# Streaming encoder layer on one core: unsplit stores for attention outputs and normed rows, in-place splits on load, low parts of weights on VectorE, two buffers for squares

## The chip, the cores and the metric

The kernel runs on one core of one Trainium2 chip. The metric is device time in microseconds (us) for one execution of the whole program; the comparison is by the median of several executions. Engine names are those of the profile: PE is TensorE's matmul stream, PEld its weight loads, DVE is VectorE, ACT is ScalarE, POOL is GpSimd, SP is SyncE. In this kernel SP issues all large transfers.

## The reference

One layer of a streaming encoder, in float32, for a prompt of 2048 rows and a sample of 32 rows with model width 1024 (2080 columns together):

```
h  = rmsnorm(x);  qa,ka,va,qb,kb,vb,g_low,r = split(h @ w_in)
oa = chunk-band attention(qa,ka,va)        # 8 heads x 64, own chunk and 8 before
ob = gated linear attention(qb,kb,vb,...)  # 4 heads, key 64, value 128
x  = x + rmsnorm(concat(oa, norm(ob)*g*silu(r)) @ w_o)
mk, mv = rmsnorm(mem) @ w_mk, rmsnorm(mem) @ w_mv          # 256 memory tokens
x  = x + rmsnorm(attention(rmsnorm(x) @ w_mq, mk, mv) @ w_mo)   # 4 heads x 256
h2 = rmsnorm(x)
x  = x + rmsnorm((silu(h2 @ w_gate) * (h2 @ w_up)) @ w_down)    # hidden 2816
```

It returns the new rows, the newest keys and values, the states of the linear attention and the memory keys and values.

## The kernel before

**Products.** Data lie feature-major: 128 features on the partitions, rows of the sequence along the free axis. A float32 operand is used as two parts, a high part, which is a rounded copy, and a low part, which is the operand less its high part; a product is three matmuls (high by high, high by low, low by high), issued at L485. `split` (L426, L430) makes the parts: ACT casts the high one (L426), and DVE or POOL subtracts for the low one (L430). Which of the two subtracts is the list `lo_set`, gone through in turn: POOL and DVE alternate in the projections, in cross attention and in the FFN, POOL alone in the stage between. Projections and FFN products multiply 2 by 2 blocks in seven products (X, Y, Z are their sums in PSUM); the combinations of weight blocks that this needs are additions and subtractions on DVE (L529, L532).

**Stages of the profiled execution.** Projections of three column blocks, 0 to 609 us (`wva`, `wvb`, `wqa`, `wka`, `wr`, `wqb`, `wkb` are their weights, `mi` the normed input in two parts). Then, 609 to 1425 us, band attention, the linear attention, the memory's keys and values, the output projection (`wops<-om,wo_s`, four column blocks) and the first memory query. Cross attention, 1425 to 1915 us, goes over five blocks of 416 columns (`m` the normed rows, `wmq`, `wmo` weights, `mpr` the exponentials of the scores). The FFN, 1915 to 3374 us, has three column blocks of 11 groups: gate (`pg<-mf,wg_s`), up (`pu<-mf,wu_s`) and down (`pdn<-u,wd`); `mf` is the normed input in two parts, `acc` the output block, two halves at a time.

**What passes through memory.** Attention outputs go to `od` and the normed rows of the first residual to `h1d`, each stored as a high and a low array and loaded as both: `om` loads `od` (128 x 2 x 512), `hq` and `m` load `h1d`. The names that are split for this are `o`/`os` and `g_sg`/`g_obs` (for `od`) and `y`/`h` (for `h1d`): an ACT cast, a POOL subtraction and two stores for each tile. The normed rows of the FFN go unsplit through `h2d` (L1704) and come back as `hr` (L1754).

**Order of issue.** The class `Order` reads every instruction of the program, gives each a time from a formula (`_cost`, L84), and runs a list scheduler forward and backward, `PASSES` times; the best schedule's order is written into the program as the order of issue on each engine, SP's queue included. Each engine then takes its instructions strictly in that order and waits at the head of its queue.

**End of an FFN block.** Squares of the output (`sq`, one buffer, L1854) are summed on DVE into `ssq` (L532); a matmul with ones gives `n_ps` (L1889), ACT makes the factor `n_r` (L434, L435), DVE multiplies it into `acc` (L1896, 16 tiles), and POOL adds the residual (`x2r`). Until a half of `acc` is stored, the next block's first results (`acc<-pdn`, L571) for that half wait.

Of the kernel before, what the change touches and what calls it, by code (L numbers as in the profile page):

```python
# [18 lines left out]
P = 128  # L19
D = 1024  # L20
# [27 lines left out]
class Order:  # L48
# [8 lines left out]
    GATE = 5  # L57
    SLOW = 1.0
    PASSES = 6

# [23 lines left out]
    def _cost(self, ins, kind, eng, outs, inps):  # L84
# [169 lines left out]
    def _pass(self, prio, back=None):  # L254
# [35 lines left out]
        while True:  # L290
            again = True
            while again:
                again = False
                for e, heap in enumerate(ready):
                    while idle[e] and heap:
# [27 lines left out]
                        if back is None:  # L323
                            seen = fin + lat[i]
                            if e == 4:
                                moved = max(moved, fin) + lat[i]
                                seen = max(fin + 2800.0, moved + 2500.0)
                            end[i] = seen
                            heappush(events, (seen, 1, i))
                        else:  # L330
                            end[i] = fin
# [4 lines left out]
            while events and events[0][0] <= now:  # L336
# [7 lines left out]
                for j in nxt[i]:  # L344
                    same = eng[j] == eng[i] and eng[i] != 4
                    if back is None:
                        if same == (kind == 0):
                            left[j] -= 1
                            if not left[j]:
                                heappush(ready[eng[j]], (prio[j], j))  # L350
                    else:
                        left[j] -= 1
                        if not left[j]:
                            heappush(events, (now + (0.0 if same else 3000.0 if eng[j] == 4 else lat[j]), 2, j))
                if last:
# [38 lines left out]
def encoder_step(ctx, tc, ins, outs):  # L394
# [26 lines left out]

    flip = [0]
    lo_set = [[nc.gpsimd, nc.vector, nc.gpsimd]]

    def split(hi, lo, src, lo_eng=None):
        ACT.copy(hi, src)  # L426
        if lo_eng is None:
            flip[0] += 1
            lo_eng = lo_set[0][flip[0] % len(lo_set[0])]
        lo_eng.tensor_tensor(out=lo, in0=src, in1=hi.bitcast(F32), op=ALU.subtract)  # L430

    def rstd_of(pool, ps_ap, n, count, name, bufs=2):
        r = pool.tile([P, n], F32, tag="rstd", name=name, bufs=bufs)
        ACT.activation(r, ps_ap, AF.Ln, bias=eps_t, scale=1.0 / count)  # L434
        ACT.activation(r, r, AF.Exp, scale=-0.5)  # L435
        return r
# [67 lines left out]
    sgd = [dpool.tile([512, n], F32, name=f"sgd{b}") for b, (_, n) in enumerate(PBLK)]  # L504
    od = [dpool.tile([D, 2, n], F32, name=f"od{b}") for b, (_, n) in enumerate(BLK)]
    x1d = [dpool.tile([D, n], F32, name=f"x1d{b}") for b, (_, n) in enumerate(BLK)]
    h1d = [dpool.tile([D, 2, n], F32, name=f"h1d{b}") for b, (_, n) in enumerate(BLK)]
    mkd = dpool.tile([D, NMEM], F32, name="mkd")
# [64 lines left out]

    lo_set[0] = [POOL, DVE]
    WCH = 1056
# [369 lines left out]

    lo_set[0] = [POOL]
    wph = ctx.enter_context(ExitStack())
    wp = wph.enter_context(tc.tile_pool(name="wpool", bufs=4, **RW))
    with ExitStack() as ph:
# [52 lines left out]
        def load_mov(src, n, name, order=range(KT)):  # L1002
            mv = {}
            for k in order:
                mv[k] = mp.tile([P, 2, 544], F32R, tag="mov", name=f"{name}_{k}")
                SP.dma_start(mv[k][:, :, :n].bitcast(F32), src[k * P : (k + 1) * P])
            return mv
# [67 lines left out]

        def heads_out(dst, osb, n, name):

            hi = lp.tile([P, 256], F32R, tag="osr", name=name, bufs=2)
            split(hi[:, :n], osb[:, :n].bitcast(F32R), osb[:, :n], POOL)
            SP.dma_start(dst[:, 0], hi[:, :n].bitcast(F32))  # L1080
            SP.dma_start(dst[:, 1], osb[:, :n])

        nbs = {}
# [14 lines left out]
        def band_group(t0, c):  # L1098
# [17 lines left out]
            def unit(tt, e):  # L1116
# [22 lines left out]
                def third():  # L1139
                    if e == 0:  # L1140
                        g["po"] = po_.tile([P, 512], F32, tag="po", name=f"po{t}_{c}")
                    values(g["po"], g["v"][:, k0 // P : k0 // P + nkt], u["prt"], [P] * nkt, e, P)
                    if e:
                        take(g["osb"][:, tt * P : (tt + 1) * P], g["po"], P, f"rec{t}_{c}")
                        if tt:
                            (b, lo, hi, _), = pieces(BLK, t0 * P, t0 * P + 256)
                            heads_out(od[b][c * P : (c + 1) * P, :, lo:hi], g["osb"], 256, f"os{t}_{c}")

# [4 lines left out]
        def band_sample(c):  # L1153
# [20 lines left out]
            def unit(e):  # L1174
# [12 lines left out]
                def third():  # L1187
# [19 lines left out]
        def gla_tile(tk, n, st, name):  # L1207
# [117 lines left out]
            DVE.tensor_tensor(out=sg[:, :, :n], in0=tts[:, :, :n], in1=sg[:, :, :n], op=ALU.mult)  # L1325
            hi = gp.tile([P, 4, P], F32R, tag="obs", name=name + "_obs")
            split(hi[:, :, :n], sg[:, :, :n].bitcast(F32R), sg[:, :, :n], POOL)
            for i, src in enumerate((hi.bitcast(F32), sg)):
                SP.dma_start(od[b][512:1024, i, lo:hi_].rearrange("(h p) n -> p h n", p=P), src[:, :, :n])

# [14 lines left out]
        def out_proj(b):  # L1345
# [101 lines left out]
        def mem_q0():  # L1447
# [277 lines left out]
    with ExitStack() as ph:  # L1725
# [92 lines left out]
        for b, (s, n) in enumerate(CF):  # L1818
# [28 lines left out]
            def square(ci, m):  # L1847
# [37 lines left out]
            def finish(ci, xrs, b=b, s=s, n=n, acc=acc, ssqs=ssqs, last=b == len(CF) - 1, load_x2=load_x2):  # L1885
# [155 lines left out]
```

## Time and profile before

| | |
|---|---|
| median of 3 executions | 3371.97 us (3369.83 to 3383.44) |
| the profiled execution | 3376.22 us |
| its span, first to last instruction | 3374.4 us |
| mean granted TensorE clock | 0.970 |
| bytes moved by DMA | 520.42 MB |
| POOL's low parts of FFN weights (`wu_s`, `wg_s`, `wd`) | 205.2, 149.0, 91.5 us busy |
| SP queue, rows in the order of issue | 1757 |

In the quoted rows, the first number of a timeline row is the start in us from the span's start and the second the time it took; a square bracket is the idle time of that engine just ahead, with what ended it. A row of a table by windows has the window, its length, then busy us and count of PE, PEld, DVE, ACT and POOL, then the granted clock of TensorE (1.00 is full), the DMA engines' share and GB/s. A row of a group has busy us and the mean ns of one, then the idle time of the engine just before them and its releasers.

### The profile page before, as it was taken

Reading aid. Unit: us, or ns where it says so; the run is one execution under the profiler, and the core shown is the slowest. Engines: PE = TensorE matmul, PEld = TensorE weight load, DVE = VectorE, ACT = ScalarE, POOL = GpSimd, SP = SyncE. Lnnn points to the kernel's source line nnn. Section 1 sums busy time; section 2 is a strip of 40 time slices with the busy share of each in tenths; the row PEclk is TensorE's granted clock in tenths of the full one; section 3 lists DMA queues with packets and bytes.
Section 4 is the critical chain, followed back from the end, with each engine's and each line's share of the span. In section 5 each row is a group of like instructions: output and inputs, shape, how many; then the busy total and the mean of one; then the engine's idle time right before and its main releaser. Section 6 shows DMA issues by size and latency. Waiting matters only on the chain. (4 is left out here: it accounts for less than half of the span.)

```text
span 3374.4 us, 58279 instructions
## 1 busy us (share of the span) xinstructions
PE 3201.7 (95%) x21387; PEld 3046.6 (90%) x21387; DVE 2350.8 (70%) x4089; ACT 1725.3 (51%) x3718; POOL 1568.0 (46%) x1331
## 2 busy tenths in 40 slices
PE   7888999899999999889999799999989999899998
PEld 6788899788888788889999689999989999899998
DVE  7884865477677677377776886666876667866665
ACT  4554655465676666455556453334533334543334
POOL 3653533274345546554451654444454445544442
PEclk8999999799999999999999899999999999999999
DMA  5549364687586867877664632222242222322222
GB/s 140 170 130 298 115 192 129 226 257 230 181 286 194 256 193 233 279 241 226 198 187 129 199 118 76 76 77 73 91 143 76 75 76 76 117 88 75 76 76 93
DMA packets 520111, 520.42 MB, mean 154 GB/s; under 512 B 81936, under 2 KB 450745, under 8 KB 519825
## 3 DMA queue, kind: packets, MB, share of 16 engines
q1 hardware_dynamic: 519825, 516.70, 48.8%
q8 instruction: 168, 2.75, 0.3%
q14 instruction: 118, 0.97, 0.1%
HBM read 386.82 MB, written 130.87 MB: 153 GB/s over the span
## 5 line engine op out<-in xcount | busy, mean ns | idle before, releaser
L485 PE MATMUL pdn<-u,wd 128*128 128x346 f32 (+1 forms) x3168 | 521.8, 324 | 18.3 <-DVE acc L571 13.2
L485 PEld LDWEIGHTS pdn<-u,wd 128*128 128x128 f32 x3168 | 510.5, 190 | 21.1 <-DVE acc L571 14.7
L426 ACT CAST wg_s<-wg_r 128x512 fp32r<-128x512 f32 x231 | 139.5, 620 | 449.9 <-DVE wg_r L529 161.4
L430 POOL TENSOR_TENSOR wu_s<-wu_r,wu_s 128x512 fp32r<-128x512 f32 x132 | 205.2, 1563 | 276.0 <-ACT wu_s L426 244.9
L532 DVE TENSOR_TENSOR acc<-acc,pdn 128x346 f32<-128x346 f32 (+1 forms) x464 | 236.0, 514 | 136.5 <-PE pdn L485 136.0
L430 POOL TENSOR_TENSOR wg_s<-wg_r,wg_s 128x512 fp32r<-128x512 f32 x99 | 149.0, 1507 | 331.2 <-ACT wg_s L426 329.9
L485 PE MATMUL pg_X<-mf,wg_s 128*128 128x346 f32 (+1 forms) x1584 | 279.1, 323 | 18.0 <-ACT wg_s L426 14.9
L485 PE MATMUL pu_X<-mf,wu_s 128*128 128x346 f32 (+1 forms) x1584 | 275.9, 321 | 0.8 <-POOL wu_s L430 0.8
L485 PEld LDWEIGHTS pg_X<-mf,wg_s 128*128 128x128 f32 x1584 | 257.3, 189 | 20.9 <-ACT wg_s L426 15.6
L485 PEld LDWEIGHTS pu_X<-mf,wu_s 128*128 128x128 f32 x1584 | 256.0, 189 | 1.8 <-POOL wu_s L430 1.4
L1340 PE MATMUL wops<-om,wo_s 128*128 128x512 f32 (+1 forms) x960 | 225.2, 373 | 12.6 <-ACT wo_s L426 6.7
L485 PE MATMUL mops<-mo,wmo_s 128*128 128x416 f32 x960 | 200.0, 357 | 3.2 <-DVE y L1684 3.2
L1340 PEld LDWEIGHTS wops<-om,wo_s 128*128 128x128 f32 x960 | 156.6, 197 | 36.0 <-ACT wo_s L426 7.5
L485 PEld LDWEIGHTS mops<-mo,wmo_s 128*128 128x128 f32 x960 | 178.8, 190 | 7.2 <-ACT n_sq L445 3.5
L426 ACT CAST wu_s<-wu_r 128x512 fp32r<-128x512 f32 x231 | 134.3, 619 | 67.1 <-DVE wu_r L529 33.8
L1064 PE MATMUL po<-prt,v 128*128 128x128 f32 x1120 | 164.7, 287 | 2.8 <-DVE o L1074 2.3
L430 POOL TENSOR_TENSOR u<-sg,u 128x346 fp32r<-128x346 f32 (+1 forms) x132 | 140.0, 1071 | 52.5 <-ACT u L426 52.5
L485 PE MATMUL mqps<-m,wmq_s 128*128 128x416 f32 x768 | 161.4, 356 | 0.0
L1064 PEld LDWEIGHTS po<-prt,v 128*128 128x128 f32 x1120 | 150.3, 199 | 11.4 <-DVE o L1074 2.7
L485 PE MATMUL pu_Y<-mf,wu_s 128*128 128x346 f32 (+1 forms) x792 | 140.8, 323 | 7.1 <-ACT wu_s L426 4.6
L485 PEld LDWEIGHTS mqps<-m,wmq_s 128*128 128x128 f32 x768 | 140.0, 189 | 1.7 <-issue 0.5
L485 PE MATMUL pg_Y<-mf,wg_s 128*128 128x346 f32 (+1 forms) x792 | 138.4, 322 | 2.1 <-POOL wg_s L430 1.4
(476 smaller groups left out, 7949.7 us busy)
## 6 DMA issues: line engine op xcount, KB each, us to landing
wg_r<-in_w_ffn_gate_dram SPq DMA_DIRECT2D x66, 512.0 KB, 4.3
wu_r<-in_w_ffn_up_dram SPq DMA_DIRECT2D x66, 512.0 KB, 4.3
wd_r<-in_w_ffn_down_dram SPq DMA_DIRECT2D x66, 512.0 KB, 3.4
wmq_r<-in_w_mq_dram SPq DMA_DIRECT2D x80, 256.0 KB, 3.0
wmo_r<-in_w_mo_dram SPq DMA_DIRECT2D x80, 256.0 KB, 3.4
q<-qd SPq DMA_DIRECT2D x32, 512.0 KB, 4.3
wo_r<-in_w_o_dram SPq DMA_DIRECT2D x64, 256.0 KB, 4.3
om<-od SPq DMA_DIRECT2D x24, 512.0 KB, 8.2
```

The lines of the kernel that those rows point to most:

```text
L426: ACT.copy(hi, src)
L430: lo_eng.tensor_tensor(out=lo, in0=src, in1=hi.bitcast(F32), op=ALU.subtract)
L485: PE.matmul(ps, lhsT=a, rhs=b, start=first and i == 0, stop=last and i == len(seq) - 1, skip_group_check=skip)
L532: eng.tensor_tensor(out=out, in0=a, in1=b, op=ALU.add)
L1064: PE.matmul(po[:, e * P : e * P + n], lhsT=v[:kk, j, e * 64 : e * 64 + P], rhs=prt[:kk, j, :n], start=j == 0, stop=j == len(rows) - 1)
L1340: PE.matmul(ps, lhsT=a, rhs=b, start=i == 0, stop=i == len(seq) - 1)
```

## The change

1. `split` always subtracts on DVE unless an engine is named; `lo_set` is gone. By the order of issue some 620 subtractions go from POOL to DVE, among them `wu` 132, `wg` 99, `wd` 66, `wo` 64, `wmq` 48, `wmo` 40, and 21 each of `wva`, `wvb`, `wqa`, `wka`, `wr`.
2. `od` and `h1d` are stored unsplit. The casts and subtractions for them (48 for `od`, 32 for `h1d`, and those of the sample) go, and so does one of each two stores.
3. The loads `om` (32 tiles), `hq` (8) and `m` fetch one array and split it in place (`split_own`): an ACT cast, then a subtraction on DVE for even tiles and on POOL for odd ones.
4. Squares at the end of an FFN block have two buffers. The factor `r` no longer has a buffer of its own but takes one of these two.
5. The planner's numbers: `SLOW`, `PASSES`, the cost of a transfer and the latencies it assumes for one.

```diff
-    SLOW = 1.0
-    PASSES = 6
+    SLOW = 1.02
+    PASSES = 7
-            return 560.0, 1.05 * total / row * (8 + 0.148 * row) / 16
+            return 540.0, total / row * (8 + 0.18 * row) / 16
-                                seen = max(fin + 2800.0, moved + 2500.0)
+                                seen = max(fin + 2500.0, moved + 2200.0)
 ...
     def split(hi, lo, src, lo_eng=None):
         ACT.copy(hi, src)
-        if lo_eng is None:
-            flip[0] += 1
-            lo_eng = lo_set[0][flip[0] % len(lo_set[0])]
-        lo_eng.tensor_tensor(out=lo, in0=src, in1=hi.bitcast(F32), op=ALU.subtract)
+        (lo_eng or DVE).tensor_tensor(out=lo, in0=src, in1=hi.bitcast(F32), op=ALU.subtract)
+    def split_own(m, on_pool):
+        ACT.copy(m[:, 0], m[:, 1].bitcast(F32))
+        (POOL if on_pool else DVE).tensor_tensor(out=m[:, 1], in0=m[:, 1].bitcast(F32), in1=m[:, 0].bitcast(F32), op=ALU.subtract)
 ...
-                SP.dma_start(mv[k][:, :, :n].bitcast(F32), src[k * P : (k + 1) * P])
+                SP.dma_start(mv[k][:, 1, :n].bitcast(F32), src[k * P : (k + 1) * P])
+                split_own(mv[k][:, :, :n], k % 2)
 ...
-            hi = lp.tile([P, 256], F32R, tag="osr", name=name, bufs=2)
-            split(hi[:, :n], osb[:, :n].bitcast(F32R), osb[:, :n], POOL)
-            SP.dma_start(dst[:, 0], hi[:, :n].bitcast(F32))
-            SP.dma_start(dst[:, 1], osb[:, :n])
+                            SP.dma_start(od[b][c * P : (c + 1) * P, lo:hi], g["osb"])
 ...
-                    hi = sp.tile([P, 544], F32R, tag="st", name=f"h1_{b}_{k}")[:, :n]
-                    split(hi, ys[k].bitcast(F32R), ys[k], POOL)
-                    SP.dma_start(h1d[b][k * P : (k + 1) * P, 0], hi.bitcast(F32))
-                    SP.dma_start(h1d[b][k * P : (k + 1) * P, 1], ys[k])
+                    SP.dma_start(h1d[b][k * P : (k + 1) * P, :], ys[k])
 ...
-                    sq = small(np_, "nsq", f"sq{b}_{ci}_{m}", 1)[:, :n]
+                    sq = small(np_, "nsq", f"sq{b}_{ci}_{m}", 2)[:, :n]
-                r = rstd_of(np_, psn[:, :n], n, D, f"n5_{b}_{ci}_r", 1)
+                r = rstd_of(np_, psn[:, :n], n, D, f"n5_{b}_{ci}_r", 2, "nsq", 348)
```

With other numbers and other instructions the planner writes another order. Four places of it follow; in the rows, `out<-in` are tiles, the ending number tells tiles apart, and the line numbers of the changed kernel are a little smaller (L425 is its `split`'s subtraction, L424 its cast, L429 the cast of `split_own`).

POOL's first arithmetic before, in the first projection block, is low parts of the weights `wva` and of the input `mi`:

```order
L430 TENSOR_TENSOR wva_s_279<-wva_r_272,wva_s_279 128x528
L430 TENSOR_TENSOR mi_5_261<-x_10_189,mi_5_261 128x4x256
L430 TENSOR_TENSOR mi_3_255<-x_11_193,mi_3_255 128x4x256
L430 TENSOR_TENSOR wva_s_289<-wva_r_272,wva_s_289 128x528
L430 TENSOR_TENSOR wva_s_297<-wva_r_272,wva_s_297 128x528
```

In the changed kernel DVE has the weights' low parts there, in one queue with the combinations (L529):

```order
L425 TENSOR_TENSOR wva_s_297<-wva_r_272,wva_s_297 128x528
L529 TENSOR_TENSOR wva_r_268<-wva_r_270,wva_r_268 128x2x264
L529 TENSOR_TENSOR wva_r_272<-wva_r_274,wva_r_272 128x2x264
L425 TENSOR_TENSOR mi_1_247<-x_00_187,mi_1_247 128x4x256
L425 TENSOR_TENSOR wva_s_302<-wva_r_268,wva_s_302 128x528
L425 TENSOR_TENSOR wva_s_305<-wva_r_272,wva_s_305 128x528
L425 TENSOR_TENSOR wva_s_308<-wva_r_268,wva_s_308 128x528
```

POOL keeps only `mi_5` and `mi_3` at this place; its next arithmetic is a sum for the norm of the second block.

ACT before, at the start of cross attention, where the last column block's normed rows are split (`h<-y`) between the exponentials (`mpr`):

```order
L426 CAST h_3_2_16943<-y_3_1_16332 128x544
L426 CAST h_3_3_16949<-y_3_1_16332 128x544
L426 CAST h_3_4_16955<-y_3_2_16333 128x544
L426 CAST h_3_5_16961<-y_3_2_16333 128x544
L1652 ACTIVATE mpr_2_1_17404,mst_2_1_17402<-ms_2_1_17395,mst_2_1_17402 104x256
L1658 COPY prT_1_17237<-mpt_1_3_17302 128x2x104
```

ACT at the same exponential in the changed kernel:

```order
L1639 ACTIVATE mpr_2_0_17143,mst_2_0_17141<-ms_2_0_17134,mst_2_0_17141 104x256
L1645 COPY prT_1_16993<-mpt_1_3_17058 128x2x104
L1639 ACTIVATE mpr_2_1_17160,mst_2_1_17158<-ms_2_1_17151,mst_2_1_17158 104x256
L424 CAST q_7_17270<-qf_7_17268 128x416
L424 CAST wmo_0_4_s<-wmo_0_4_r 128x512
L1645 COPY prT_2_17133<-mpt_2_0_17147 128x2x104
```

The casts of `h` are gone from between the exponentials.

SP before, ahead of the FFN, where the normed rows of the fourth block of cross attention are stored (`h2d`) and loads of `hr` for the second FFN block are already planned:

```order
L1704 DMA h2d_123<-y_3_5_21883 128x416
L1704 DMA h2d_123<-y_3_6_21920 128x416
L1754 DMA hr_00_26075<-h2d_121 128x4x136
L1704 DMA h2d_123<-y_3_7_21957 128x416
L1754 DMA hr_00_26075<-h2d_122 128x4x210
```

SP there in the changed kernel:

```order
L1691 DMA h2d_123<-y_3_5_21687 128x416
L1691 DMA h2d_123<-y_3_6_21724 128x416
L1691 DMA h2d_123<-y_3_7_21761 128x416
L1741 DMA hr_00_25879<-h2d_121 128x4x136
L1741 DMA hr_00_25879<-h2d_122 128x4x210
```

The last store has come ahead of the first of these loads.

PE before, between the first and the second FFN block, with the two sums for the norm (`n_0_1_ps`, `n_0_0_ps`) among `pu_1` and `pdn_0` of the next block:

```order
L1889 MATMUL n_0_1_ps<-ssq_1_27118,ones 128x348
L485 MATMUL pu_1_Y<-mf_1_26929,wu_1_s_27735 128x346 x7
...
L485 MATMUL pdn_0_4_1_27940<-u_0_1_27548,wd_1_1_27905 128x346 x3
L1889 MATMUL n_0_0_ps<-ssq_0_27205,ones 128x348
L485 MATMUL pdn_0_5_1_27948<-u_0_0_27547,wd_0_1_27897 128x346 x3
```

PE there in the changed kernel:

```order
L1876 MATMUL n_0_1_ps<-ssq_1_26922,ones 128x348
L485 MATMUL pg_1_Z<-mf_5_26747,wg_1_s_27424 128x346 x12
...
L485 MATMUL pu_1_Z<-mf_5_26747,wu_1_s_27553 128x346 x12
L1876 MATMUL n_0_0_ps<-ssq_0_27009,ones 128x348
L485 MATMUL pu_1_X<-mf_6_26751,wu_1_s_27556 128x346 x12
L485 MATMUL pdn_0_0_1_27712<-u_0_0_27351,wd_0_0_27698 128x346 x3
```

Both sums now stand ahead of the first `pdn` of the next block.

More of the change, by code (lines that the diff above doesn't have):

```diff
@@ L353, in _pass @@
                         if not left[j]:
-                            heappush(events, (now + (0.0 if same else 3000.0 if eng[j] == 4 else lat[j]), 2, j))
+                            heappush(events, (now + (0.0 if same else 2700.0 if eng[j] == 4 else lat[j]), 2, j))
                 if last:
@@ L420, in load_gain, with rstd_of @@
         gains[gname] = gt
-    flip = [0]
-    lo_set = [[nc.gpsimd, nc.vector, nc.gpsimd]]
     def split(hi, lo, src, lo_eng=None):
         ACT.copy(hi, src)
-        if lo_eng is None:
-            flip[0] += 1
-            lo_eng = lo_set[0][flip[0] % len(lo_set[0])]
-        lo_eng.tensor_tensor(out=lo, in0=src, in1=hi.bitcast(F32), op=ALU.subtract)
-    def rstd_of(pool, ps_ap, n, count, name, bufs=2):
-        r = pool.tile([P, n], F32, tag="rstd", name=name, bufs=bufs)
+        (lo_eng or DVE).tensor_tensor(out=lo, in0=src, in1=hi.bitcast(F32), op=ALU.subtract)
+    def split_own(m, on_pool):
+        ACT.copy(m[:, 0], m[:, 1].bitcast(F32))
+        (POOL if on_pool else DVE).tensor_tensor(out=m[:, 1], in0=m[:, 1].bitcast(F32), in1=m[:, 0].bitcast(F32), op=ALU.subtract)
+    def rstd_of(pool, ps_ap, n, count, name, bufs=2, tag="rstd", width=None):
+        r = pool.tile([P, width or n], F32, tag=tag, name=name, bufs=bufs)[:, :n]
         ACT.activation(r, ps_ap, AF.Ln, bias=eps_t, scale=1.0 / count)
@@ L504, in encoder_step @@
     sgd = [dpool.tile([512, n], F32, name=f"sgd{b}") for b, (_, n) in enumerate(PBLK)]
-    od = [dpool.tile([D, 2, n], F32, name=f"od{b}") for b, (_, n) in enumerate(BLK)]
+    od = [dpool.tile([D, n], F32, name=f"od{b}") for b, (_, n) in enumerate(BLK)]
     x1d = [dpool.tile([D, n], F32, name=f"x1d{b}") for b, (_, n) in enumerate(BLK)]
-    h1d = [dpool.tile([D, 2, n], F32, name=f"h1d{b}") for b, (_, n) in enumerate(BLK)]
+    h1d = [dpool.tile([D, n], F32, name=f"h1d{b}") for b, (_, n) in enumerate(BLK)]
     mkd = dpool.tile([D, NMEM], F32, name="mkd")
@@ L571, in out @@
             f(*a)
-    lo_set[0] = [POOL, DVE]
     WCH = 1056
@@ L943, in encoder_step @@
             SP.dma_start(outs["av_t"].rearrange("t (c e d) -> t c e d", c=4, e=2)[:, :, e], vad[-1][256:, :, 2 * e])
-    lo_set[0] = [POOL]
     wph = ctx.enter_context(ExitStack())
@@ L1074, in take @@
                 DVE.tensor_tensor(out=dst[own], in0=po[own, e * P : e * P + n], in1=rec[own, :n], op=ALU.mult)
-        def heads_out(dst, osb, n, name):
-            hi = lp.tile([P, 256], F32R, tag="osr", name=name, bufs=2)
-            split(hi[:, :n], osb[:, :n].bitcast(F32R), osb[:, :n], POOL)
-            SP.dma_start(dst[:, 0], hi[:, :n].bitcast(F32))
-            SP.dma_start(dst[:, 1], osb[:, :n])
         nbs = {}
@@ L1146, in third @@
                             (b, lo, hi, _), = pieces(BLK, t0 * P, t0 * P + 256)
-                            heads_out(od[b][c * P : (c + 1) * P, :, lo:hi], g["osb"], 256, f"os{t}_{c}")
+                            SP.dma_start(od[b][c * P : (c + 1) * P, lo:hi], g["osb"])
                 return first, second, third
@@ L1192, in third @@
                         take(g["osb"][:, :TS], g["po"], TS, f"srec_{c}")
-                        heads_out(od[-1][c * P : (c + 1) * P, :, 512:], g["osb"], TS, f"sos_{c}")
+                        SP.dma_start(od[-1][c * P : (c + 1) * P, 512:], g["osb"][:, :TS])
                 return first, second, third
@@ L1325, in gla_tile @@
             DVE.tensor_tensor(out=sg[:, :, :n], in0=tts[:, :, :n], in1=sg[:, :, :n], op=ALU.mult)
[L1326 to L1329, printed above, removed]
+            SP.dma_start(od[b][512:1024, lo:hi_].rearrange("(h p) n -> p h n", p=P), sg[:, :, :n])
         def states_out():
@@ L1456, in first @@
                     mv[k] = pl.tile([P, 2, w], F32R, tag=tag, name=f"hq0_{k}", **kw)
-                    SP.dma_start(mv[k][:, :, :n].bitcast(F32), h1d[0][k * P : (k + 1) * P, :, :n])
+                    SP.dma_start(mv[k][:, 1, :n].bitcast(F32), h1d[0][k * P : (k + 1) * P, :n])
+                    split_own(mv[k][:, :, :n], k % 2)
             def query(m):
@@ L1563, in encoder_step @@
             it()
-    lo_set[0] = [POOL, DVE]
     with ExitStack() as ph:
@@ L1600, in mem_h @@
                 for bb, lo, hi, off in pieces(BLK, s, s + n):
-                    SP.dma_start(m_[:, :, off : off + hi - lo].bitcast(F32), h1d[bb][k * P : (k + 1) * P, :, lo:hi])
+                    SP.dma_start(m_[:, 1, off : off + hi - lo].bitcast(F32), h1d[bb][k * P : (k + 1) * P, lo:hi])
+                split_own(m_, k % 2)
                 mv.append(m_)
```

## The prediction

> **What bounds the kernel now.** I read the busy shares and the chain first, then the table by windows, then the groups, and last the timelines around the longest idle times of PE.
>
> ```profile
> PE 3201.7 (95%) x21387; PEld 3046.6 (90%) x21387; DVE 2350.8 (70%) x4089; ACT 1725.3 (51%) x3718; POOL 1568.0 (46%) x1331
> PE 39%; DVE 2%; ACT 1%; issue 0%; POOL 0%; DVEq 0%; ACTq 0%; POOLq 0%
> ...
> 30.00:170.00 140.00, 121.19 (x880) 111.36 (x879) 117.13 (x141) 78.88 (x162) 73.18 (x52) 0.95 0.52 156
> 170.00:400.00 230.00, 209.69 (x1306) 202.39 (x1307) 162.27 (x203) 124.82 (x236) 104.38 (x69) 0.95 0.63 195
> 609.00:820.00 211.00, 195.10 (x1708) 168.40 (x1707) 145.06 (x416) 128.98 (x365) 102.36 (x150) 0.91 0.75 239
> 1330.00:1425.00 95.00, 86.53 (x547) 82.96 (x547) 29.65 (x35) 41.97 (x79) 59.37 (x45) 0.93 0.88 291
> 2100.00:2300.00 200.00, 200.00 (x1257) 200.00 (x1256) 130.50 (x207) 76.41 (x148) 82.48 (x63) 1.00 0.25 79
> 2300.00:2462.00 162.00, 156.01 (x972) 154.33 (x970) 133.91 (x176) 79.56 (x144) 79.54 (x55) 1.00 0.31 98
> ```
>
> PE is busy for 95% of the span, and no matmul is removed. So the most that the change can win is PE's idle time, 3374.4 - 3201.7 = 172.7 us, and what low clock costs beside it. In the FFN's steady stretch (2100 to 2300) PE is busy for all of the 200 us at full clock: there faster DVE or POOL work is worth nothing. What can be won lies in the projections (18.8 us idle in 30 to 170, 20.3 in 170 to 400), in the stage after them, and at seams.
>
> **Low parts on DVE.** Two engines slow each other when they subtract at once:
>
> ```profile
> L430 POOL TENSOR_TENSOR wu_s<-wu_r,wu_s 128x512 fp32r<-128x512 f32 x132 | 205.2, 1563 | 276.0 <-ACT wu_s L426 244.9 <-issue 19.7 <-PE pg_Z L485 11.0
> L430 DVE TENSOR_TENSOR wu_s<-wu_r,wu_s 128x512 fp32r<-128x512 f32 x99 | 100.3, 1034 | 22.0 <-ACT wu_s L426 21.9
> L529 DVE TENSOR_TENSOR wu_r<-wu_r 128x512 f32<-128x512 f32 x33 | 42.1, 1276 | 36.1 <-POOL wu_s L430 36.1
> 2318.54 0.69 DVE L430 TENSOR_TENSOR wg_s<-wg_r,wg_s 128x512 fp32r<-128x512 f32 x1
> 2319.33 1.37 DVE L529 TENSOR_TENSOR wg_r<-wg_r 128x512 f32<-128x512 f32 x1
> 2319.22 0.94 POOL L430 TENSOR_TENSOR u<-sg,u 128x348 fp32r<-128x348 f32 x1 [1.32 <-ACT u L426]
> ```
>
> A 128x512 operation takes DVE 0.69 us with POOL idle and 1.37 us beside a POOL operation, and DVE's `wu_s` average 1.03. The moved operations cost POOL 1.56 us and will cost DVE 0.69, so 620 of them add at most 620 x 0.69 = 428 us to DVE; against that, each freed DVE from an overlap worth up to 1.37 - 0.69 = 0.68 us. If half of the 620 overlapped, that returns 211 us, and DVE gains about 217 us to some 2570 of 3374 (76%). The bounds are +6 (all overlapped) and +428 (none, 82%); neither fills DVE over the whole span. By windows the fullest is 2300 to 2462: 133.9 us busy of 162. A group takes 44 us there ((3374 - 1915) / 33), so it holds some 4, each handing over 9 low parts (132 + 99 + 66 over 33 groups): at the mean return of half, 36 x (0.69 - 0.34) = 13 us, to 147 of 162, under PE's 156. The cover there is PE's own work on the group before. If it fails, `acc<-acc,pdn`, queued behind the low parts on DVE, holds PSUM and PE waits for it.
>
> The Trainium skill ("SBUF — State Buffer", section "Who interferes with whom") says that a DVE instruction with two inputs in SBUF and a GpSimd instruction that reads SBUF shut each other out for a whole instruction; by that, 1.37 is 0.69 of waiting and 0.69 of work, and the trace agrees. The Trainium skill ("Perfetto Trace Analysis", section "Optimizing Scalar/DVE Operations") also says that where DVE is saturated, moving work to Scalar or GPSIMD may make sense, and adds that the shared port may spoil it: its first half speaks against this change where DVE is fullest, and by it the time would go the way of rival (a), whose price is worked out there from rows.
>
> Where this reaches PE is the projections. At the start:
>
> ```profile
> 16.20 6.39 DVE L642 SCALAR_TENSOR_TENSOR x<-x,g_pre_mix,xr 128x256 f32<-128x256 f32 x8 [0.20 <-ACT xr L637]
> 23.25 3.47 DVE L529 TENSOR_TENSOR wva_r<-wva_r 128x528 f32<-128x528 f32 x2
> 19.00 2.52 POOL L430 TENSOR_TENSOR mi<-x,mi 128x1024 fp32r<-128x1024 f32 x1
> 23.27 0.81 PE L485 MATMUL wva_X<-wva_s,mi 128*128 128x264 f32 x2 [5.33 <-DVE wva_s L430]
> 29.14 4.77 PE L485 MATMUL wva_X<-wva_s,mi 128*128 128x264 f32 x20 [5.07 <-DVE mi L430]
> ```
>
> DVE's queue sets both waits (10.4 us), and part of it is slow beside POOL. POOL keeps `mi` there, so the eight `x` stay slow beside 2.5 us of it, but `wva_r` runs at 0.7 instead of 1.7 each. DVE also takes over two low parts ahead of that `mi` (2 x 0.7). From 23 to 48 us DVE does 21 operations, of which I count about 8 us of overlap time; it takes on 7 x 0.7 = 4.9. Net about 3 us, and POOL's late `wva_s` (1.3 to 1.7 each after ACT's cast) become 0.7: I take -5, between +5 (nothing returned) and -10. In the rest of 30 to 400 us, of 39.1 us idle, 10.1 wait for a transfer (`fl<-biasd`) that stays as it is, and the low parts of five weights set perhaps a third of the rest: -8, between +10 and -15.
>
> In the stage after them (609 to 1330), the idle time in its first window is 211.0 - 195.1 = 15.9 us at a clock of 0.91. `wo`'s low parts (64) move and about 100 POOL subtractions vanish, while 40 loads are split. I take -5, between +12 and -15.
>
> **Unsplit stores.** The clearest stall is where the last normed rows are split:
>
> ```profile
> 1476.22 0.54 PE L485 MATMUL ms<-kTp,q 128*104 128x256 f32 x1 [9.78 <-ACT mpr L1652]
> 1473.76 0.65 ACT L426 CAST h<-y 128x544 fp32r<-128x544 f32 x1 [2.26 <-POOL y L430]
> 1475.06 0.64 ACT L426 CAST h<-y 128x544 fp32r<-128x544 f32 x1 [0.65 <-POOL y L430]
> 1475.61 0.47 ACT L1652 ACTIVATE mpr<-ms,mst 104x256 f32<-104x256 f32 x1
> 1464.18 6.64 POOL L430 TENSOR_TENSOR y<-y,h 128x544 fp32r<-128x544 f32 x2 [4.10 <-ACT h L426]
> 1476.00:1485.00 9.00, 8.13 (x35) 7.58 (x36) 5.23 (x14) 5.13 (x17) 4.71 (x4) 0.50 0.77 263
> ```
>
> ACT's exponential stands behind casts of `h`, these wait for POOL to free a staging tile, and POOL's two take 6.64 us since DVE runs beside it. PE loses 9.8 us, and for the next 9 us its clock is 0.50, which costs 4.5 more. Casts, subtractions and staging tiles all go. Next in line is DVE's split of `q`, about 1.3 us, so I take -12 of the 14.3; the ends are 0 (another wait in its place) and -14.
>
> Bytes: `od` and `h1d` hold 1024 x 2080 x 4 = 8.5 MB each per part. Two stores and two loads lose one part each, 34 MB of 520.42. Where DMA binds is 1330 to 1425 us (share 0.88):
>
> ```profile
> om<-od SPq DMA_DIRECT2D x24, 512.0 KB, 8.2
> 1357.81 0.62 ACT L426 CAST wo_s<-wo_r 128x512 fp32r<-128x512 f32 x1 [2.99 <-DMA wo_r<-in_w_o_dram]
> 1362.51 0.62 ACT L426 CAST h<-y 128x512 fp32r<-128x512 f32 x1 [1.22 <-DMA h1d<-h]
> L1340 PE MATMUL wops<-om,wo_s 128*128 128x272 f32 x384 | 56.5, 310 | 8.5 <-ACT wo_s L426 6.7 <-POOL wo_s L430 1.1 <-DVE y L1381 0.3
> ```
>
> PE's 8.5 us there come from `wo` landing late and from ACT's queue. With less traffic and no `h` in that queue I take -5, between 0 and -8.
>
> **New casts on load.** 72 ACT casts now wait for transfers at the head of ACT's queue; one takes 0.62 us, 45 us in all, and the removed casts (48 + 32 and the sample's) give back as much. Their subtractions fall on DVE (36) and POOL (36). The price is a cast standing before its load has landed: `om` took 8.2 us with both parts. Were ACT held for half of that once per column block, 4 x 4.1 = 16 us; hidden, 0. Nearest is the wait of 2.99 us for `wo_r`; I take one such, +3.
>
> **SP's order at the FFN's start.**
>
> ```profile
> 1915.07 2.83 PE L485 MATMUL pg_X<-mf,wg_s 128*128 128x348 f32 x8 [13.86 <-ACT wg_s L426]
> 1914.40 0.62 ACT L426 CAST wg_s<-wg_r 128x512 fp32r<-128x512 f32 x1 [7.57 <-DMA h2d<-y]
> 1910.66 0.37 SPq L1754 DMA_DIRECT2D hr<-h2d  x1
> 1911.08 0.50 SPq L1704 DMA_DIRECT2D h2d<-y  x1
> 1906.09 4.54 DVE L430 TENSOR_TENSOR mf<-hr,mf 128x1392 fp32r<-128x1392 f32 x1
> ```
>
> ACT waits for the last `h2d` store, which stands on SP behind a load of `hr`; that load waits for DVE's `mf` to free its tile. In the new order the store is ahead of the load and can go 5.9 us earlier than 1911.1 (after the previous stores end near 1901.6, its `y` being ready by 1905.2). I take -6 of the 13.9, between 0 and -9.
>
> **Squares and the seams of the FFN.**
>
> ```profile
> 2470.73 9.76 PE L485 MATMUL pdn<-u,wd 128*128 128x346 f32 x48 [6.04 <-DVE acc L571]
> 2464.56 5.68 DVE L1896 SCALAR_TENSOR_TENSOR acc<-acc,g_post_ffn,n_r 128x348 f32<-128x348 f32 x6 [2.02 <-ACT n_r L435]
> ```
>
> Between blocks PE waits 6.0 us because `acc` is copied from PSUM only behind the second half's scaling. Two square buffers let ACT run ahead of DVE's sums, and both norm sums now precede `pdn`; but `r` must wait for a square's buffer. Over two seams I take -5, between +6 (the 16 scalings in one run, behind which the copies queue) and -12.
>
> **Sum.** -5 - 8 - 5 - 12 - 5 + 3 - 6 - 5 = -43 us on 3376.2, the profiled execution, so 3333. That execution lies 4.2 above the median of 3372.0; beside the median the sum is 3329, and I forecast 3330. The planner's numbers cost no instruction; what they do is in the order shown. A run and its neighbours differ by up to 0.4%, so 0.5% (17 us) is what can be told from no change: the limits are 3355 and 3389.
>
> **Rivals.** (a) DVE becomes the bound in the projections. It is busy there for 117 of 140 and 162 of 230 us, and takes over 126 low parts (five weights of 21, `wkb` 12, `wqb` 9) in the 609 us. Each that PE waits for at its full length costs 0.69 us; the other terms give -30. It decides from 30 / 0.69 = 44 of the 126 (no gain) and from 68 (measurably slower); with two in three, 84 x 0.69 = 58, the sum is +28, or 3400. For it: DVE's `wva_s` and `mi` are PE's releasers at the start. Against it: 0.69 on DVE ends sooner than 1.56 on POOL, and PE's wait is for the part, not for the engine. (b) No change: the seams' waits pass to the next in line (13.9 at the FFN waits for `mf` and weights anyway, 9.8 for `q`), leaving a third of the sum, -14: 3358. (c) More: contention and low clock go in all of 0 to 1915. Half of 172.7 us idle, 86 us: 3286. (d) New casts on load hold ACT's queue: +16 in place of +3, or 3343, still faster.
>
> **Chances.** The forecast with (d) 0.60, (c) 0.12, (b) 0.17, (a) 0.11. Faster than 3355: 0.73 (a little of (b) among it); within 0.5%: 0.16; slower: 0.11. The range goes from (c), 3286, to where (a) begins to count, 3378; the likeliest alone has 3312 to 3350.
>
> **What would show it.** Right: no wait of some 10 us for `mpr` at the start of cross attention; about 8 us or less ahead of the first `pg_X`; DVE's `wu_s` near 0.7 us each and POOL busy under a third; DMA bytes near 486 MB. Wrong: DVE as the releaser of PE in the FFN's steady stretch or of `wva`; ACT waiting for `om` with PE behind it; seams of the FFN above 6 us.

## The result and the profile after

The changed kernel takes 3315.87 us (median of 4, 3312.47 to 3316.82) against 3372.51 for the kernel before: ratio 0.9824, 95% interval [0.9801, 0.9847], 56.6 us faster. The forecast was 3330 in 3286 to 3378, faster. The profiled execution took 3312.47 us.

The page of the changed kernel, its busy shares and the three groups of moved low parts that are the largest:

```profile
span 3310.7 us, 57927 instructions
PE 3173.7 (96%) x21387; PEld 3030.5 (92%) x21387; DVE 2518.5 (76%) x4760; ACT 1719.1 (52%) x3706; POOL 633.0 (19%) x647
DMA packets 490076, 486.31 MB, mean 147 GB/s; under 512 B 78528, under 2 KB 427881, under 8 KB 489793
L425 DVE TENSOR_TENSOR wu_s<-wu_r,wu_s 128x512 fp32r<-128x512 f32 x231 | 155.5, 697 | 26.4 <-ACT wu_s L424 26.4
L425 DVE TENSOR_TENSOR wg_s<-wg_r,wg_s 128x512 fp32r<-128x512 f32 x231 | 166.4, 726 | 1.8 <-ACT wg_s L424 1.6
L425 DVE TENSOR_TENSOR wd<-wd_r,wd 128x512 fp32r<-128x512 f32 x132 | 103.4, 786 | 114.2 <-ACT wd L424 114.2
```

POOL loses 935 us of work (1568.0 to 633.0; some of it is the subtractions of part 2 that vanish) and DVE gains only 168 (2350.8 to 2518.5): a low part of `wu` takes 0.70 us where DVE averaged 1.03 and POOL 1.56. PE's idle time falls from 172.7 to 3310.7 - 3173.7 = 137.0 us. That is 35.7 of the 63.7 us between the two profiled spans; the other 28.0 us are PE's busy time, for the same 21387 matmuls. The granted clock's mean went from 0.970 to 0.979. Its records hold only the values 1.00 and 0.50, so that is about 200 us at half clock before (2 x 0.030 x 3374.4) and 140 after; 60 us less at half clock are worth up to 30 us of busy time.

The same program split at the same work (first `po`, last `po`, first `mops`, last `mops`, a tenth of `pdn`), in the table by windows, before and then after:

```profile
0.00:617.90 617.90, 549.42 (x3563) 525.70 (x3564) 429.96 (x537) 322.59 (x607) 264.09 (x183) 0.95 0.57 170
617.90:1311.60 693.70, 674.08 (x5767) 577.02 (x5766) 487.73 (x1395) 451.34 (x1203) 340.51 (x450) 0.96 0.72 226
1311.60:1493.30 181.70, 161.18 (x978) 153.21 (x977) 99.74 (x143) 94.40 (x212) 126.85 (x90) 0.92 0.83 273
1493.30:1900.90 407.60, 403.81 (x2306) 389.83 (x2304) 291.61 (x471) 229.48 (x516) 179.00 (x128) 0.99 0.61 191
1900.90:2117.00 216.10, 192.19 (x1162) 185.79 (x1161) 163.51 (x222) 97.55 (x180) 105.06 (x74) 0.97 0.34 108
2117.00:3374.40 1257.40, 1221.01 (x7622) 1215.08 (x7620) 878.24 (x1325) 529.93 (x1003) 552.43 (x407) 0.99 0.27 86
```

```profile
0.00:601.60 601.60, 543.33 (x3560) 525.13 (x3561) 445.48 (x675) 322.13 (x605) 62.06 (x45) 0.96 0.58 176
601.60:1290.00 688.40, 660.98 (x5773) 566.77 (x5773) 520.22 (x1514) 439.36 (x1174) 191.93 (x311) 0.97 0.65 202
1290.00:1447.50 157.50, 149.44 (x967) 144.64 (x966) 114.41 (x184) 89.14 (x203) 47.55 (x32) 0.98 0.76 239
1447.50:1856.20 408.70, 403.83 (x2311) 388.50 (x2310) 310.19 (x552) 239.09 (x543) 100.63 (x78) 1.00 0.59 180
1856.20:2061.10 204.90, 194.75 (x1163) 189.17 (x1162) 169.13 (x260) 97.17 (x178) 39.41 (x29) 0.97 0.35 109
2061.10:3310.70 1249.60, 1221.39 (x7622) 1216.25 (x7620) 959.08 (x1578) 532.15 (x1004) 191.46 (x155) 0.99 0.27 87
```

The differences in length are -16.3, -5.3, -24.2, +1.1, -11.2 and -7.8 us. The third stage gains most: PE is 12.4 us less idle there (20.5 to 8.1), and its clock rises from 0.92 to 0.98. In the long stretches where PE was already nearly full (fourth and sixth, 99% and 97% busy), DVE's extra 18.6 and 80.8 us of work cost no time.

How far such a difference can be trusted shows in a run described below ("One row of SP's order"): up to the FFN it runs the same instructions in the same order on every engine as the kernel before. Its second and third stage were:

```profile
620.10:1308.00 687.90, 668.96 (x5766) 573.35 (x5766) 489.48 (x1395) 451.48 (x1203) 341.44 (x450) 0.97 0.72 227
1308.00:1492.80 184.80, 161.81 (x979) 153.00 (x978) 95.53 (x143) 94.34 (x212) 126.60 (x90) 0.93 0.82 268
```

These two are 5.8 us shorter and 3.1 us longer than before, with nothing changed. In single profiles a stage's difference below some 6 us therefore shows nothing.

The longest waits of PE in the changed kernel, from its list of waits (total, times, longest):

```profile
PE wva_X L485 <- DVE mi L425: 13.4, 4, 9.1
PE pdn L485 <- DVE acc L571: 11.4, 2, 5.7
PE mqps L485 <- DVE m L430: 7.9, 1, 7.9
```

The waits of 13.9 us ahead of the first `pg_X` and of 9.8 us for `mpr` are gone. A new one of 7.9 us for `m` has come at the start of cross attention, and the waits for `acc` at the seams stay at up to 5.7 (6.0 before).

### The profile page after: what moved, and what is told of

Read it like the earlier page. It is cut to its first block, busy times and chain, and to the rows that moved or that the text cites. A ratio compares the mean times of both kernels' runs of the same rounds, so it can differ in the third digit from the quotient of the medians.

```text
span 3310.7 us, 57927 instructions
## 1 busy us (share of the span) xinstructions
PE 3173.7 (96%) x21387; PEld 3030.5 (92%) x21387; DVE 2518.5 (76%) x4760; ACT 1719.1 (52%) x3706; POOL 633.0 (19%) x647
## 5 line engine op out<-in xcount | busy, mean ns | idle before, releaser
L485 PE MATMUL pdn<-u,wd 128*128 128x346 f32 (+1 forms) x3168 | 520.7, 324 | 15.3 <-DVE acc L571 11.4
L424 ACT CAST wg_s<-wg_r 128x512 fp32r<-128x512 f32 x231 | 139.5, 620 | 491.6 <-DVE wg_r L529 179.9
L425 POOL TENSOR_TENSOR u<-sg,u 128x346 fp32r<-128x346 f32 (+1 forms) x132 | 159.0, 1213 | 1101.9 <-ACT u L424 619.9
L1329 PE MATMUL wops<-om,wo_s 128*128 128x512 f32 (+1 forms) x960 | 212.1, 362 | 0.6 <-DVE om L430 0.5
L425 DVE TENSOR_TENSOR wd<-wd_r,wd 128x512 fp32r<-128x512 f32 x132 | 103.4, 786 | 114.2 <-ACT wd L424 114.2
L425 DVE TENSOR_TENSOR wu_s<-wu_r,wu_s 128x512 fp32r<-128x512 f32 x231 | 155.5, 697 | 26.4 <-ACT wu_s L424 26.4
L1329 PEld LDWEIGHTS wops<-om,wo_s 128*128 128x128 f32 x960 | 149.0, 189 | 21.9 <-issue 3.0
L425 DVE TENSOR_TENSOR wg_s<-wg_r,wg_s 128x512 fp32r<-128x512 f32 x231 | 166.4, 726 | 1.8 <-ACT wg_s L424 1.6
L424 ACT CAST wu_s<-wu_r 128x512 fp32r<-128x512 f32 x231 | 136.7, 619 | 59.2 <-DVE wu_r L529 39.7
L1063 PEld LDWEIGHTS po<-prt,v 128*128 128x128 f32 x1120 | 146.9, 199 | 16.3 <-ACT g_W L1237 3.5
```

Of the source, the lines that this page charges most:

```text
L425: (lo_eng or DVE).tensor_tensor(out=lo, in0=src, in1=hi.bitcast(F32), op=ALU.subtract)
L485: PE.matmul(ps, lhsT=a, rhs=b, start=first and i == 0, stop=last and i == len(seq) - 1, skip_group_check=skip)
L1063: PE.matmul(po[:, e * P : e * P + n], lhsT=v[:kk, j, e * 64 : e * 64 + P], rhs=prt[:kk, j, :n], start=j == 0, stop=j == len(rows) - 1)
L1329: PE.matmul(ps, lhsT=a, rhs=b, start=i == 0, stop=i == len(seq) - 1)
```

## The experiments

Two theories were set against each other. P: each part pays at its own place (low parts in the projections and at the FFN's start, unsplit stores between the attention stage and cross attention). O: what pays is the order that the planner happens to write (it plans anew for every kernel in the table). Times are medians; each ratio is to the kernel before, run beside it, with its 95% interval.

| kernel | us | ratio |
|---|---|---|
| low parts on DVE alone | 3338.49 | 0.9899 [0.9877, 0.9921] |
| unsplit stores alone | 3354.27 | 0.9945 [0.9926, 0.9964] |
| planner's numbers alone | 3386.39 | 1.0042 [1.0030, 1.0054] |
| squares alone | 3369.73 | 0.9992 [0.9978, 1.0006] |
| changed, less low parts on DVE | 3365.87 | 0.9981 [0.9970, 0.9992] |
| changed, less unsplit stores | 3343.08 | 0.9911 [0.9893, 0.9929] |
| changed, less planner's numbers | 3308.32 | 0.9808 [0.9788, 0.9828] |
| changed, less squares | 3322.67 | 0.9848 [0.9831, 0.9866] |

**Low parts on DVE, alone and taken away.**

```diff
-        lo_eng.tensor_tensor(out=lo, in0=src, in1=hi.bitcast(F32), op=ALU.subtract)
+        (lo_eng or DVE).tensor_tensor(out=lo, in0=src, in1=hi.bitcast(F32), op=ALU.subtract)
```

> The kernel before with part 1 alone: every low part without a named engine on DVE. Theory P (each part pays at its own place): the projections win their 17 us (block 2 starts at about 400 us instead of 418), the start of the FFN some 10 of its 13.9 us wait, the 9.8 us wait for mpr stays; 3340 to 3350 us. Theory O (what pays is the order that the planner writes; a part alone only shuffles waits): within 10 us of 3372, with new waits of 5 us and more where old ones went.

> The changed kernel with part 1 undone: low parts alternate between POOL and DVE (POOL alone in the attention stage), all else as changed. Theory P: it loses what part 1 gives, 22 to 32 us, 3338 to 3348, with the loss in the projections and at the start of the FFN. Theory O: within 10 us of 3316, or a loss at other places.

Alone it wins 35.4 us (3373.86 beside it); taken away from the changed kernel it costs 50.0. By the same places as above, alone: the projections end 21.7 us earlier, the stage from the last `po` to the first `mops` wins 3.2, and from the last `mops` to a tenth of `pdn` 12.2. Taken away: the projections end 22.8 us later than in the changed kernel, and that start of the FFN is 11.1 us longer. So the places are those of theory P, but not all of its signs came. Alone, the median is 1.5 us below its range, the wait for `mpr` did not stay (2.5 us at most), and cross attention took 9.3 us more (416.9 against 407.6), which neither theory names. Taken away, the loss is larger than expected, and the FFN behind a tenth of `pdn` is 13 us longer too (1262.8 against 1249.6), a place that gains nothing when part 1 is alone. Part 1 is thus worth 15 us more in the company of the others than alone.

**Unsplit stores, alone and taken away.**

```diff
-    h1d = [dpool.tile([D, 2, n], F32, name=f"h1d{b}") for b, (_, n) in enumerate(BLK)]
+    h1d = [dpool.tile([D, n], F32, name=f"h1d{b}") for b, (_, n) in enumerate(BLK)]
```

(with all casts, subtractions, stores and loads of part 3)

> The kernel before with part 3 alone: od and h1d stored unsplit, loads split in place; low parts of weights as before. Theory P: projections unchanged within 3 us, the 9.8 us wait for mpr gone and the stretch from the last output projection to the first mops 20 to 28 us shorter; 3344 to 3352 us. Theory O: within 10 us of 3372.

> The changed kernel with part 3 undone: od and h1d stored and loaded in two parts. Theory P: it loses 20 to 28 us between the attention stage and cross attention, 3336 to 3344, and the 9.8 us wait for mpr is back. Theory O: within 10 us of 3316, or a loss at other places.

Alone -19.6 us (2 us short of theory P's range), taken away +27.2. The stage from the last `po` to the first `mops`, in the windows of four kernels (unsplit stores alone; low parts alone; changed less unsplit stores; the changed kernel is above), shows where:

```profile
1312.70:1464.10 151.40, 146.75 (x933) 140.37 (x932) 97.21 (x127) 86.58 (x194) 110.21 (x75) 0.98 0.71 227
1286.00:1464.50 178.50, 159.54 (x953) 151.16 (x952) 110.69 (x171) 90.67 (x204) 59.27 (x41) 0.92 0.82 271
1295.60:1468.60 173.00, 157.23 (x961) 149.19 (x959) 110.28 (x172) 89.72 (x203) 54.38 (x38) 0.95 0.85 280
```

In these five windows it takes 173 to 182 us with split stores, at a DMA share of 0.82 to 0.85; unsplit, 151 to 158 at 0.71 to 0.76. Alone, unsplit stores win 30.3 us here and give some of it back elsewhere (cross attention takes 412.9 instead of 407.6). What PE waits for there, in the list of waits of the changed kernel less unsplit stores:

```profile
PE wops L1338 <- ACT wo_s L424: 8.5, 5, 2.6
PE ms L485 <- ACT mpr L1649: 2.1, 3, 1.0
```

The expected return of the 9.8 us wait for `mpr` is a miss: it is 1.0 at most. Waits for `wo_s` of 8.5 us in all are what returned (9.0 with low parts on DVE alone, 6.7 before, none of this size unsplit). What ACT in turn waited for in this stage differs (the kernel before; low parts alone; the last two rows, changed less unsplit stores):

```profile
ACT wo_s L426 <- DMA wo_r<-in_w_o_dram: 13.4, 6, 4.9
ACT wo_s L424 <- DMA wo_r<-in_w_o_dram: 20.6, 9, 5.5
ACT h L424 <- DMA h1d<-h: 7.2, 5, 2.7
ACT wo_s L424 <- DMA wo_r<-in_w_o_dram: 1.8, 3, 1.1
```

In the first two kernels it is weights still on their way, which speaks for the bytes. In the third it is more the casts of `h`, which wait until a staging tile has been stored. Neither row stands in the stage's list of the changed kernel. So it is shown that unsplit stores take the stall away, but not how much of it was bytes and how much the split of the rows.

**The planner's numbers, alone and taken away.**

```diff
-    SLOW = 1.0
+    SLOW = 1.02
```

(with the other four changed lines of part 5)

> The kernel before with part 5 alone: the planner's five numbers, no instruction changed. Theory P: nothing by itself, within 8 us of 3373. Theory O: if the order is what pays, this alone wins a good part of the 57 us, 3335 to 3355.

> The changed kernel with the planner's old numbers. Theory P: within 8 us of 3316. Theory O: 15 to 40 us lost.

Alone, both theories miss: the numbers lose 13.3 us. Without them the changed kernel is at 3308.32 (3301.08 to 3310.54), just inside theory P's 8 us and against theory O. That is below all four runs of the changed kernel, but those were taken at another time, and the two ratios' intervals overlap (0.9788 to 0.9828 and 0.9801 to 0.9847). So an order written with other numbers is worth some 10 us, and these numbers aren't what paid: alone they cost. In the profile of the numbers alone, a longer wait for `mi` (5.1 at most before) and a new one stand in the projections, in the list of waits over 0 to 420 us:

```profile
PE wva_X L485 <- DVE mi L430: 11.3, 3, 9.6
PE wka_Z L485 <- DVE wqa_st L532: 6.6, 1, 6.6
```

**Squares, alone and taken away.**

```diff
-                    sq = small(np_, "nsq", f"sq{b}_{ci}_{m}", 1)[:, :n]
+                    sq = small(np_, "nsq", f"sq{b}_{ci}_{m}", 2)[:, :n]
```

> The kernel before with part 4 alone: two buffers for squares, the factor in one of them. Theory P: each seam of the FFN 2 to 4 us shorter, 3365 to 3371. Theory O: anything within 10 us, with the seams' waits of 6.0 us for acc unchanged or longer.

> The changed kernel with one buffer for squares and the factor in its own. Theory P: 3 to 8 us lost, all at the two seams of the FFN, 3319 to 3324. Theory O: within 10 us on either side, elsewhere too.

Alone it can't be told from no change; its profiled execution gains 1 us between a tenth of `pdn` and the end. Taken away it costs 6.8 us by the medians; of the 8.1 us between the two profiled spans 4.5 lie in the FFN behind a tenth of `pdn`. The times are those of theory P, but its mechanism is not what the waits for `acc` show (the kernel before; squares alone; changed less squares; the changed kernel has 11.4, 2, 5.7):

```profile
PE pdn L485 <- DVE acc L571: 13.2, 4, 6.0
PE pdn L490 <- DVE acc L576: 17.6, 4, 10.6
PE pdn L485 <- DVE acc L571: 8.3, 4, 4.1
```

With two buffers for squares these waits are longer in both pairs, as theory O had it for squares alone. Where the small cost of taking them away comes from stays open.

**One row of SP's order.** In the kernel before, the last store of `h2d` for the fourth block is put ahead of the first `hr` load of the second FFN block; nothing else moves.

```diff
         start = best[1]
+        start[store] = start[load] - 0.001   # store: last h2d3 row, load: first hr1_00 row
```

> The kernel before with one row of SP's order moved: the last store of h2d for the fourth block stands ahead of the first load of hr for the second FFN block; every other engine's order is unchanged. Theory S (SP's order held ACT's wg_s cast): the 13.9 us ahead of the first pg_X fall to 6 to 9 and the span by as much. Theory D (what held it is the last normed row, late since DVE and POOL slow each other): the wait stays above 12.

```profile
1906.07 0.95 PE L495 MATMUL pg_X<-mf,wg_s 128*128 128x348 f32 x2 [6.60 <-ACT wg_s L436]
1910.07 2.11 PE L495 MATMUL pg_X<-mf,wg_s 128*128 128x348 f32 x6 [3.05 <-DVE wg_s L440]
1904.35 4.56 DVE L440 TENSOR_TENSOR mf<-hr,mf 128x1392 fp32r<-128x1392 f32 x1
```

The wait falls from 13.86 to 6.60 us, as theory S has it, but the span doesn't: 3.05 us come back at once, since the low part of `wg_s` stands behind DVE's `mf`, which takes 4.56 us beside POOL's. From the last `mops` to a tenth of `pdn` the gain is 1.7 us (time 3374.25, one run), less than the stages ahead differ by themselves. The rest of the 11.2 us at this place needs the low parts on DVE: with them (alone, or in the changed kernel less unsplit stores) this stretch is 11 to 12 us shorter; without them (unsplit stores alone, changed less low parts) 2.4 us or nothing.

How the wait itself went in the changed kernel shows on ACT: its first cast of `wg_s` stands ahead of casts of `mf` that it stood behind before (the first three rows are of the changed kernel, the last of the kernel before, where `wg_s` follows at 1914.40):

```profile
1854.26 0.60 ACT L424 CAST wg_s<-wg_r 128x512 fp32r<-128x512 f32 x1
1856.63 2.61 ACT L424 CAST mf<-hr 128x1392 fp32r<-128x1392 f32 x2 [1.77 <-PE mops L485]
1856.43 2.08 PE L485 MATMUL pg_X<-mf,wg_s 128*128 128x348 f32 x12
1900.11 3.86 ACT L426 CAST mf<-hr 128x1392 fp32r<-128x1392 f32 x3 [1.00 <-PE mops L485]
```

Low parts on DVE alone have this order too, with the planner's old numbers. So at this place theory O is right in part: the wait goes through a new order on ACT, which the planner wrote because of part 1.

**POOL kept busy.** Low parts on DVE alone, but where POOL had one before it now does three short subtractions into a scratch tile that nobody reads (some 610 times).

```diff
+                for q in range(3):
+                    v = hi[:, q % hi.shape[1], :w].bitcast(F32)
+                    POOL.tensor_tensor(out=scr[:, :w], in0=v, in1=v, op=ALU.subtract)
```

> Low parts on DVE as in part 1 alone, and wherever POOL had one before, POOL now does three short subtractions (128 to 160 wide, about 1.4 us together) into a scratch tile that nobody reads. Theory C (part 1 pays because POOL no longer slows DVE): DVE's wu_s go back above 0.9 us, and the gain of 35 us is lost or worse, 3360 to 3400. Theory L (it pays because one low part takes 0.7 us on DVE and 1.5 on POOL, and its user gets it sooner): the scratch work costs little, 3336 to 3350.

3402.11 us, ratio 1.0088 [1.0072, 1.0103]: 64 us above low parts on DVE alone, though nobody reads the scratch tile. (The scratch work does read the high parts, and ACT's casts wait 14.0 us in all until it has.) Theory L's 3336 to 3350 is far off. Theory C's range is missed by 2 us, and one of its signs did not come: DVE's `wu_s` go up from 0.69 to 0.815 us, not above 0.9. In all, DVE's 4724 operations take 2597.4 us instead of 2510.8.

```profile
L429 DVE TENSOR_TENSOR wu_s<-wu_r,wu_s 128x512 fp32r<-128x512 f32 x231 | 182.9, 815 | 52.7 <-ACT wu_s L428 52.6
PE wva_X L491 <- DVE mi L429: 22.6, 3, 16.5
PE pg_X L491 <- ACT wg_s L428: 18.8, 2, 18.5
```

POOL is busy for 1826 us there, more than the 1568 before, and its own queue is longer too. So what is shown is that short low parts on DVE don't pay by themselves: POOL must be free as well. That they pay nothing isn't shown. How much of the 64 us is DVE slowed, how much POOL's other work standing behind the scratch work, and how much the order isn't separated. Part of it is order: the wait of 18.5 us ahead of `pg_X` runs from 1913.7 to 1932.3 us, where POOL does no scratch work, and there ACT's first cast of `wg_s` again stands behind casts of `mf`.

**Two attempts to go on**, both from the changed kernel with the planner's old numbers.

```diff
-        (POOL if on_pool else DVE).tensor_tensor(out=m[:, 1], ...)
+        DVE.tensor_tensor(out=m[:, 1], ...)
```

> The changed kernel with the planner's old numbers (3308), and all in-place low parts of loads on DVE. Theory C: the scalings of y ahead of m's low part run undisturbed, the 8 us wait of mqps for m shrinks to 3 to 5, 3298 to 3305. Theory Q (DVE's queue is what is long there): 36 more operations of 0.6 us make that wait longer, 3309 to 3320.

```diff
-        put(b22, POOL)
-        put(b21, POOL)
+        put(b22, DVE)
+        put(b21, DVE)
```

> The changed kernel with the planner's old numbers (3308), and the two low parts of each projection and FFN input (mi, mf) that POOL had on DVE as well. Theory C: the first block's waits for mi shrink by 3 to 6 us, 3300 to 3306. Theory Q: 12 more operations of 1.2 to 1.6 us in DVE's queue at the starts of blocks, where PE waits for DVE: 3309 to 3318.

3305.14 (3304.24 to 3307.01) and 3310.98 (3306.57 to 3314.99) against 3308.32 (3301.08 to 3310.54): neither can be told from its base. In the first the wait for `m` is 7.8 us against 8.0, so both theories miss it: giving DVE the half of the subtractions that POOL had doesn't touch it. The changed kernel's timeline shows what stands ahead of that `m` on DVE: five operations of 1.6 to 1.9 us, beside POOL's sums for `y` and `acc`, which the first attempt leaves where they are. The same scaling of `y` takes 0.77 us a little later:

```profile
1405.12 3.14 PE L485 MATMUL mqps<-m,wmq_s 128*128 128x416 f32 x8 [7.87 <-DVE m L430]
1401.58 1.85 DVE L1381 SCALAR_TENSOR_TENSOR y<-y,g_post_mix,acc 128x544 f32<-128x544 f32 x1
1408.32 0.77 DVE L1381 SCALAR_TENSOR_TENSOR y<-y,g_post_mix,acc 128x544 f32<-128x544 f32 x1
```

Moving those sums is untested. In the second attempt the projections end 5.4 us earlier and the first block's last matmul starts 3.1 us earlier; the first block's waits of `wva_X` for `mi` shrink by 2.5 us (5.9 to 3.4), less than theory C's 3 to 6. The seams' waits for `acc` grow from 14.4 to 25.5 us in all, as theory Q would have it. The first is 10.7 us below the changed kernel's median, with no run in common.

## Why the prediction was right, step by step

**Size and sign.** -43 us were forecast on the profiled span and 63.7 came; the sum was two thirds of it. By the medians, which the profiled executions exaggerate, 42 were forecast and 56.6 came. The mis-sized term is the clock: low clock was counted at one place, with 4.5 us, and PE's busy time fell by 28.0 us over the whole program. The idle time alone fell by 35.7 us, near the sum of the waits that were counted. Most of the 28.0 us lie in the first three stages (6.1, 13.1 and 11.7). In the projections and the third stage the idle time fell with them, as it would if each wait taken away also took away slow matmuls behind it; in the attention stage PE's idle time rose (19.6 to 27.4), so that account isn't the whole one. The total lies in the range partly by luck: as the next paragraphs show, several terms had about the right size for another reason than the one given.

**Low parts on DVE.** DVE gained 168 us (forecast 217, bounds 6 and 428), and it did not become the bound, so rival (a) did not come. (The prediction took 2300 to 2462 for its fullest window, 83% busy; 30 to 170 in its own table is fuller, 84%. In 30 to 180 us DVE goes from 127.1 to 136.1 us and PE from 129.1 to 133.2.) In the projections -13 was forecast and -16.3 came, but not as divided: PE's run of 20 `wva_X` starts at 25.65 us instead of 29.14, -3.5 for the start's -5, and more than all the rest lies in the first block (the first `wva` of the second block comes 20.5 us earlier, that of the third 14.0). The start's gain is not from the two waits that were priced: they were 10.4 us together and are 9.75 (0.62 and 9.13); PE's first `wva_X` comes 2.3 us earlier. One of the prediction's signs of being wrong did show, DVE as PE's releaser at `wva`: its longest wait for DVE's `mi` went from 5.1 to 9.1 us, though the stage is shorter. With the planner's old numbers that wait is 5.6. POOL's remaining `mi` is stretched beside DVE, but no wait of PE in this stretch is put down to it:

```profile
25.65 4.46 PE L485 MATMUL wva_X<-wva_s,mi 128*128 128x264 f32 x20 [9.13 <-DVE mi L425]
22.52 8.92 POOL L425 TENSOR_TENSOR mi<-x,mi 128x1024 fp32r<-128x1024 f32 x1 [3.02 <-ACT mi L424]
```

**Unsplit stores.** For the stage from the last `po` to the first `mops`, -12 for the split of `h`, -5 for bytes and +3 for casts were forecast, -14 together; -24.2 came. The mechanism of the first was too simple (without unsplit stores the wait for `mpr` can be as short as 1.0 us). The second, -5 for bytes and ACT's queue together, was undersized: with split stores `wops` waits 6.7 to 9.0 us for `wo_s`, and PE runs there at a clock of 0.92 to 0.95 instead of 0.98; bytes and queue are not told apart. The splits on load cost more than +3 at one place, in the direction of rival (d), yet not in ACT's queue: DVE's scalings of `y` and weights' low parts run ahead, and `mqps` waits 7.9 us for a low part of `m`.

**SP's order.** The store did move, and when that alone was done the wait fell by 7.3 us, near the 6 forecast; but alone it was worth 1.7 us. The step that failed is "can go 5.9 us earlier" taken as a gain: DVE's `mf` and `wg_s` were the next in line. That 11.2 us came is due to the low parts, and to the new place of ACT's `wg_s` cast that came with them, which the prediction did not look at.

**Squares.** -5 was forecast, and the whole change made the stretch behind a tenth of `pdn` 7.8 us shorter. The step that failed is that two buffers shorten the wait for `acc`: it stays at up to 5.7 us a seam, and in both pairs of runs it is longer with two buffers. The wait of `n_ps` for `ssq` went, 3.9 us in all, but it is gone in the changed kernel with one buffer as well. The nearness of -5 and -7.8 is luck.

**The planner's numbers** were priced at nothing; alone they cost 13.3 us, and perhaps 8 in the changed kernel.

**The attention stage** (-5 forecast, -5.3) agrees in size, but the same instructions in the same order gave -5.8 there once: the agreement shows nothing.

## What to carry to other kernels

Where two engines share work that they slow each other at, moving it all to the faster one can cost that engine far less than the work moved: with low parts on DVE alone, 880 us left POOL (1568.0 to 688.2) and 160 came to DVE (2350.8 to 2510.8). Price an idle gap with the slow clock behind it, not by its length alone. And a wait that is taken away is worth only what the next in line leaves: look for it on every engine that the waiting instruction needs, and look where the new order of issue has put that instruction.

## What the hardware showed that I had not expected

A DVE instruction can be held up for nearly the whole of a POOL instruction beside it, and POOL is held up by DVE too. In the changed kernel DVE's low part of `wd`, 128x512, takes 0.69 us alone and 3.44 beside a POOL subtraction of 128x1384 that takes 3.25:

```profile
2304.19 0.69 DVE L425 TENSOR_TENSOR wd<-wd_r,wd 128x512 fp32r<-128x512 f32 x1
2305.98 3.44 DVE L425 TENSOR_TENSOR wd<-wd_r,wd 128x512 fp32r<-128x512 f32 x1
2305.62 3.25 POOL L425 TENSOR_TENSOR mf<-hr,mf 128x1384 fp32r<-128x1384 f32 x1 [19.16 <-ACT mf L424]
```

And POOL's `mi`, 2.5 us elsewhere, took 8.92 beside back-to-back DVE work. The Trainium skill ("SBUF — State Buffer", section "Who interferes with whom") has this as an exclusive lock held for an instruction; the 3.44 us agree with it, and by that rule the 8.92 fit only if the one that waits can lose the lock several times in a row, which no run here tests.
